# Larger loads, fewer buffers, one output tile: a weighted sum of expert outputs on one core

## The chip, the cores and the metric

The kernel runs on one core of a Trainium2 chip. The metric is the device time of one execution in microseconds (us): the median of three runs of the kernel before is 721.33 us, with runs from 721.21 to 722.09. The profile that is read below is one execution taken by the hardware profiler; its span is 720.4 us. In its lines DVE is VectorE, ACT is ScalarE, POOL is GpSimd and SP is SyncE; a "q" behind an engine's name (SPq) is the part of the engine that issues its transfers, and q1, q10 and q0 are the DMA queues of SyncE, ScalarE and GpSimd.

## The reference

For each of 16 x 1024 = 16384 tokens there are the outputs of 8 experts, each a vector of 512 float32 values, and 8 weights. The result is the weighted sum of the 8 vectors.

```python
batch, seq, n_experts, expert_dim = 16, 1024, 8, 512

def reference(expert_outputs, combine_weights):
    weights = combine_weights[..., np.newaxis]
    return np.sum(expert_outputs * weights, axis=2).astype(np.float32)
```

268.4 MB of expert outputs and 0.5 MB of weights are read and 33.6 MB are written. There is no reuse: every value of the input is multiplied once and added once.

## The kernel before

The tokens are spread over 128 partitions. A step takes 256 tokens, J = 2 neighbouring tokens in each partition, so a load is 4 MiB: one row of 32 KiB (2 tokens x 8 experts x 512 x 4 bytes) for each partition. Loads go alternately to the queues of SyncE and ScalarE, three steps ahead, into four buffers. The 8 KB of weights of a step are loaded by GpSimd, into four small buffers. The output of a step goes to one of four output tiles and is stored on the queue that did not load this step.

```python
in_pool = ctx.enter_context(tc.tile_pool(name="in_pool", bufs=4))
w_pool = ctx.enter_context(tc.tile_pool(name="w_pool", bufs=4))
out_pool = ctx.enter_context(tc.tile_pool(name="out_pool", bufs=4))
prod_pool = ctx.enter_context(tc.tile_pool(name="prod_pool", bufs=2))
...                                        # ES = 4, K_TAIL = 2, LA = 3
load_engines = [nc.sync, nc.scalar]

def issue_load(m):
    in_t = in_pool.tile([P, J, E, D], fp32, name="in_t")
    w_t = w_pool.tile([P, J, E], fp32, name="w_t")
    if m < n_steps - K_TAIL:
        load_engines[m % 2].dma_start(out=in_t, in_=eo_blk[m])
    else:                                  # the last two steps: a transfer for each j
        ...
    nc.gpsimd.dma_start(out=w_t, in_=w_blk[m])
```

The sum of a token is a chain of eight VectorE instructions on 128 x 512 float32 values: a multiply (line 77 in the profile), and then seven times a fused multiply and add (line 83).

```python
for n in range(n_steps):
    if n + LA < n_steps:
        issue_load(n + LA)
    if n >= n_steps - K_TAIL:
        continue
    acc = out_pool.tile([P, J, D], fp32)
    for j in range(J):
        nc.vector.tensor_scalar_mul(out=acc[:, j, :], in0=in_tile[:, j, 0, :],
                                    scalar1=w_tile[:, j, 0:1])
        for e in range(1, E):
            nc.vector.scalar_tensor_tensor(
                out=acc[:, j, :], in0=in_tile[:, j, e, :],
                scalar=w_tile[:, j, e : e + 1], in1=acc[:, j, :],
                op0=mybir.AluOpType.mult, op1=mybir.AluOpType.add)
    load_engines[(n + 1) % 2].dma_start(out=o_blk[n], in_=acc)
```

In the last two steps the work is shared: ScalarE multiplies experts 4 to 7 into bf16 products, VectorE sums experts 0 to 3 and then adds the products, and each j is stored on its own. The buffers synchronise themselves: a tile taken from a pool may be written once all that used its buffer before, a store that reads it among them, has ended.

Of the kernel before, what the change touches and what calls it, by code (L numbers as in the profile page):

```python
# [1 line left out]

# [4 lines left out]


@with_exitstack  # L10
def kernel(
    ctx: ExitStack,
    tc: tile.TileContext,
    expert_outputs: bass.AP,
    combine_weights: bass.AP,
    out: bass.AP,
):
    nc = tc.nc
    fp32 = mybir.dt.float32
    bf16 = mybir.dt.bfloat16  # L20

    B, S, E, D = expert_outputs.shape
    T = B * S
    P = 128
    J = 2
    n_steps = T // (P * J)

    eo_blk = expert_outputs.rearrange("b s e d -> (b s) e d").rearrange(
        "(n p j) e d -> n p j e d", p=P, j=J
    )  # L30
    w_blk = combine_weights.rearrange("b s e -> (b s) e").rearrange(
        "(n p j) e -> n p j e", p=P, j=J
    )
    o_blk = out.rearrange("b s d -> (b s) d").rearrange(
        "(n p j) d -> n p j d", p=P, j=J
    )

    in_pool = ctx.enter_context(tc.tile_pool(name="in_pool", bufs=4))
    w_pool = ctx.enter_context(tc.tile_pool(name="w_pool", bufs=4))
    out_pool = ctx.enter_context(tc.tile_pool(name="out_pool", bufs=4))  # L40
    prod_pool = ctx.enter_context(tc.tile_pool(name="prod_pool", bufs=2))

    ES = E // 2
    K_TAIL = 2

    load_engines = [nc.sync, nc.scalar]

    LA = 3
    in_tiles: list[bass.AP | None] = [None] * n_steps
    w_tiles: list[bass.AP | None] = [None] * n_steps  # L50

    def issue_load(m: int) -> None:
        in_t = in_pool.tile([P, J, E, D], fp32, name="in_t")
        w_t = w_pool.tile([P, J, E], fp32, name="w_t")
        if m < n_steps - K_TAIL:
            load_engines[m % 2].dma_start(out=in_t, in_=eo_blk[m])
        else:
            for j in range(J):
                load_engines[m % 2].dma_start(out=in_t[:, j], in_=eo_blk[m, :, j])
        nc.gpsimd.dma_start(out=w_t, in_=w_blk[m])  # L60
        in_tiles[m] = in_t
        w_tiles[m] = w_t

    for m in range(min(LA, n_steps)):
        issue_load(m)

    for n in range(n_steps):
        if n + LA < n_steps:
            issue_load(n + LA)
        if n >= n_steps - K_TAIL:  # L70
            continue
        in_tile = in_tiles[n]
        w_tile = w_tiles[n]
        acc = out_pool.tile([P, J, D], fp32)

        for j in range(J):
            nc.vector.tensor_scalar_mul(  # L77
                out=acc[:, j, :],
                in0=in_tile[:, j, 0, :],
                scalar1=w_tile[:, j, 0:1],  # L80
            )
            for e in range(1, E):
                nc.vector.scalar_tensor_tensor(  # L83
                    out=acc[:, j, :],
                    in0=in_tile[:, j, e, :],
                    scalar=w_tile[:, j, e : e + 1],
                    in1=acc[:, j, :],
                    op0=mybir.AluOpType.mult,
                    op1=mybir.AluOpType.add,
                )  # L90

        load_engines[(n + 1) % 2].dma_start(out=o_blk[n], in_=acc)  # L92

    tail_steps = list(range(n_steps - K_TAIL, n_steps))
    tail_accs = {}
    tail_prods = {}
    for n in tail_steps:
        acc = out_pool.tile([P, J, D], fp32, name="acc")
        prods = prod_pool.tile([P, J, E - ES, D], bf16, name="prods")
        tail_accs[n] = acc  # L100
        tail_prods[n] = prods

    for j in range(J):
        for n in tail_steps:
            in_tile = in_tiles[n]
            w_tile = w_tiles[n]
            acc = tail_accs[n]
            prods = tail_prods[n]

            for e in range(ES, E):  # L110
                nc.scalar.mul(  # L111
                    out=prods[:, j, e - ES, :],
                    in_=in_tile[:, j, e, :],
                    mul=w_tile[:, j, e : e + 1],
                )
            nc.vector.tensor_scalar_mul(  # L116
                out=acc[:, j, :],
                in0=in_tile[:, j, 0, :],
                scalar1=w_tile[:, j, 0:1],
            )  # L120
            for e in range(1, ES):
                nc.vector.scalar_tensor_tensor(  # L122
                    out=acc[:, j, :],
                    in0=in_tile[:, j, e, :],
                    scalar=w_tile[:, j, e : e + 1],
                    in1=acc[:, j, :],
                    op0=mybir.AluOpType.mult,
                    op1=mybir.AluOpType.add,
                )
            nc.vector.tensor_add(  # L130
                out=prods[:, j, 0:2, :],
                in0=prods[:, j, 0:2, :],
                in1=prods[:, j, 2:4, :],
            )
            nc.vector.tensor_add(  # L135
                out=prods[:, j, 0, :], in0=prods[:, j, 0, :], in1=prods[:, j, 1, :]
            )
            nc.vector.tensor_add(  # L138
                out=acc[:, j, :], in0=acc[:, j, :], in1=prods[:, j, 0, :]
            )  # L140
            nc.sync.dma_start(out=o_blk[n, :, j], in_=acc[:, j, :])


# [1 line left out]
_INS = ['expert_outputs', 'combine_weights']  # L145
_OUTS = [((16, 1024, 512), 'float32')]


# [23 lines left out]
```

## Time and profile before

| what | value |
|---|---|
| time, median of 3 | 721.33 us |
| span of the profiled execution | 720.4 us |
| VectorE busy | 644.4 us, 1020 instructions |
| ScalarE busy | 11.4 us |
| bytes moved | 302.63 MB, mean 420 GB/s |
| load of 4 MiB, issue to landing | 33.3 us (SyncE), 33.5 us (ScalarE) |
| store of 512 KB, issue to landing | 33.4 us (SyncE), 33.5 us (ScalarE) |
| weights of a step, issue to landing | 6.9 us |
| last stores of 256 KB, issue to landing | 3.0 us |

A group of instructions in the page reads: line, engine, operation, what it writes and reads, shape and count, then the busy time in us and the mean duration of one in ns, then the idle time of the engine just before such instructions and what ended most of it. Successive VectorE instructions overlap a little, so that the busy time is less than count times duration. In the table of stretches a row has the stretch and its length, the busy time and count of VectorE, ScalarE and GpSimd, the clock of TensorE (not used here), the share of time in which the 16 DMA engines were busy, and what they moved in GB/s. The "chain of waits" follows the work that ended last back to what released it, step by step.

### The profile page before, as it was taken

What the parts mean: (1) busy time and instruction counts of PE and PEld (TensorE: products, weight loads), DVE (VectorE), ACT (ScalarE), POOL (GpSimd) and SP (SyncE); (2) the same over time, 40 slices, a digit from 0 to 9 for tenths busy, and PEclk for the clock granted to TensorE, in tenths of its full rate; (3) what the DMA queues carried; (4) which work ended last, traced back from release to release, by engine and by line L of the source; (5) the groups of instructions that cost most, each with busy time, mean ns of one, the idle gap of its engine ahead of it and who ended that gap; (6) DMA issues with size and microseconds to landing.
All of it is one profiled execution on the core that took longest, in us unless ns stands there. A gap on an engine that the chain in (4) does not pass through costs nothing.

```text
span 720.4 us, 1532 instructions
## 1 busy us (share of the span) xinstructions
DVE 644.4 (89%) x1020; ACT 11.4 (2%) x17; POOL 35.8 (5%) x68
## 2 busy tenths in 40 slices
DVE  0799999999998999989998999989998999999977
ACT  0000000000000000000000000000000000000023
POOL 1000000000000000000000000000000000000000
DMA  9999999999999999999999999999999999999993
GB/s 380 437 416 451 427 426 430 427 424 439 443 431 426 426 423 431 438 436 434 431 423 426 435 430 442 432 424 427 430 429 432 442 431 428 430 425 428 433 359 120
DMA packets 21068, 302.63 MB, mean 420 GB/s; under 512 B 3136, under 2 KB 4160, under 8 KB 12608
## 3 DMA queue, kind: packets, MB, share of 16 engines
q1 hardware_dynamic: 9792, 151.52, 49.2%
q10 hardware_dynamic: 9216, 150.47, 48.9%
q0 software_dynamic: 2048, 0.53, 0.3%
q14 instruction: 12, 0.10, 0.0%
HBM read 268.96 MB, written 33.55 MB: 420 GB/s over the span
## 4 chain that ended last, share of the span: by engine, by line
DMA 63%; DVE 35%; issue 1%; DVEq 0%; SPq 0%
DMA out_dram<-acc 56%; DVE acc L83 30%; DMA in_t<-in_expert_outputs_dram 8%; DVE acc L77 3%; DVE acc L122 1%; DVE acc L138 0%; DVE prods L130 0%; DVE acc L116 0%; DVE prods L135 0%; DVEq L77 0%; DVEq L116 0%; SPq L92 0%
## 5 line engine op out<-in xcount | busy, mean ns | idle before, releaser
L83 DVE SCALAR_TENSOR_TENSOR acc<-in_t,w_t,acc 128x512 f32<-128x512 f32 x868 | 580.1, 743 | 0.0
L77 DVE TENSOR_SCALAR acc<-in_t,w_t 128x512 f32<-128x512 f32 x124 | 54.6, 482 | 66.3 <-DMA in_t<-in_expert_outputs_dram 43.4
L60 POOL DMA_DIRECT2D w_t<-in_combine_weights_dram x64 | 35.6, 556 | 637.7 <-DVE acc L83 636.9
L111 ACT ACT_TABLE_LOAD x1 | 1.3, 1283 | 690.6 <-DMA in_t<-in_expert_outputs_dram 690.6
L111 ACT ACTIVATE prods<-in_t,w_t 128x512 bf16<-128x512 f32 x16 | 10.1, 709 | 9.0 <-DMA in_t<-in_expert_outputs_dram 9.0
L122 DVE SCALAR_TENSOR_TENSOR acc<-in_t,w_t,acc 128x512 f32<-128x512 f32 x12 | 8.9, 745 | 0.0
L116 DVE TENSOR_SCALAR acc<-in_t,w_t 128x512 f32<-128x512 f32 x4 | 1.9, 481 | 5.3 <-DMA out_dram<-acc 5.3
L138 DVE TENSOR_TENSOR acc<-acc,prods 128x512 f32<-128x512 f32 x4 | 2.8, 688 | 0.0
L130 DVE TENSOR_TENSOR prods<-prods 128x1024 bf16<-128x1024 bf16 x4 | 2.7, 683 | 0.0
L135 DVE TENSOR_TENSOR prods<-prods 128x512 bf16<-128x512 bf16 x4 | 1.7, 417 | 0.0
L156 POOL MEMSET const-float32-0.0<- 128x1 f32 x1 | 0.1, 99 | 0.2 <-issue 0.2
L156 POOL MEMSET const-bfloat16-1.0<- 128x1 bf16 x1 | 0.1, 102 | 0.0
L156 POOL MEMSET const-float32-1.0<- 128x1 f32 x1 | 0.1, 99 | 0.0
L156 POOL MEMSET const-uint8-127<- 128x1 uint8 x1 | 0.1, 99 | 0.0
## 6 DMA issues: line engine op xcount, KB each, us to landing
in_t<-in_expert_outputs_dram ACTq DMA_DIRECT2D x31, 4096.0 KB, 33.5
in_t<-in_expert_outputs_dram SPq DMA_DIRECT2D x31, 4096.0 KB, 33.3
out_dram<-acc ACTq DMA_DIRECT2D x31, 512.0 KB, 33.5
out_dram<-acc SPq DMA_DIRECT2D x31, 512.0 KB, 33.4
in_t<-in_expert_outputs_dram SPq DMA_DIRECT2D x2, 2048.0 KB, 31.2
in_t<-in_expert_outputs_dram ACTq DMA_DIRECT2D x2, 2048.0 KB, 13.9
w_t<-in_combine_weights_dram POOLq DMA_DIRECT2D x64, 8.0 KB, 6.9
out_dram<-acc SPq DMA_DIRECT2D x4, 256.0 KB, 3.0
```

Source lines behind the costliest of these rows:

```text
L60: nc.gpsimd.dma_start(out=w_t, in_=w_blk[m])
L77: nc.vector.tensor_scalar_mul(out=acc[:, j, :], in0=in_tile[:, j, 0, :], scalar1=w_tile[:, j, 0:1],)
L83: nc.vector.scalar_tensor_tensor(out=acc[:, j, :], in0=in_tile[:, j, e, :], scalar=w_tile[:, j, e : e + 1], in1=acc[:, j, :], op0=mybir.Al ...
L111: nc.scalar.mul(out=prods[:, j, e - ES, :], in_=in_tile[:, j, e, :], mul=w_tile[:, j, e : e + 1],)
L116: nc.vector.tensor_scalar_mul(out=acc[:, j, :], in0=in_tile[:, j, 0, :], scalar1=w_tile[:, j, 0:1],)
L122: nc.vector.scalar_tensor_tensor(out=acc[:, j, :], in0=in_tile[:, j, e, :], scalar=w_tile[:, j, e : e + 1], in1=acc[:, j, :], op0=mybir.Al ...
L130: nc.vector.tensor_add(out=prods[:, j, 0:2, :], in0=prods[:, j, 0:2, :], in1=prods[:, j, 2:4, :],)
L135: nc.vector.tensor_add(out=prods[:, j, 0, :], in0=prods[:, j, 0, :], in1=prods[:, j, 1, :])
L138: nc.vector.tensor_add(out=acc[:, j, :], in0=acc[:, j, :], in1=prods[:, j, 0, :])
L156: nc = _bacc.Bacc("TRN2", target_bir_lowering=False, num_devices=1)
```

## The change

- A chunk is now 512 tokens, J = 4 in each partition, and a load is 8 MiB, one row of 64 KiB for each partition. All loads go to SyncE's queue. There are three input buffers, and two chunks are loaded ahead.
- All weights are loaded once, at the start, by ScalarE's queue, into one tile: 8 rows of 512 bytes for each partition.
- The first multiply of each token moves from VectorE to ScalarE. VectorE does seven fused operations for each token.
- There is one output tile instead of four. To give VectorE something to do while the store of the chunk before still reads that tile, the first token of a chunk is summed in place, in its input buffer; only its last operation writes to the output tile. ScalarE does the first multiply of the next chunk (`first`) ahead of issuing the store.
- The last seven loads are cut into pieces that become smaller, down to one expert of one token for each partition in the very last, so that the sum can follow the data closely. The bf16 products of the last steps go.

The three input buffers (64 KiB for each partition), the output tile (8 KiB) and the weights (4 KiB) take 204 KiB for each partition.

```diff
-    J = 2
-    n_steps = T // (P * J)
+    K = 16
+    J = 4
+    N = T // (P * K)
...
+    x = expert_outputs.rearrange("b s e d -> (b s) e d").rearrange(
+        "(n p k) e d -> n p (k e) d", p=P, k=K
+    )
+    w = combine_weights.rearrange("b s e -> (b s) e").rearrange(
+        "(n p k) e -> p n (k e)", p=P, k=K
+    )
...
-    in_pool = ctx.enter_context(tc.tile_pool(name="in_pool", bufs=4))
-    w_pool = ctx.enter_context(tc.tile_pool(name="w_pool", bufs=4))
-    out_pool = ctx.enter_context(tc.tile_pool(name="out_pool", bufs=4))
-    prod_pool = ctx.enter_context(tc.tile_pool(name="prod_pool", bufs=2))
+    in_pool = ctx.enter_context(tc.tile_pool(name="in_pool", bufs=3))
+    w_pool = ctx.enter_context(tc.tile_pool(name="w_pool", bufs=1))
+    out_pool = ctx.enter_context(tc.tile_pool(name="out_pool", bufs=1))
...
+    chunks = [(n, k) for n in range(N) for k in range(0, K, J)]
+    last = len(chunks) - 1
...
+    def cuts(i):
+        if i == last:
+            return (0, 4, 8, 12, 16, 20, 24, 26, 28, 29, 30, 31, 32)
+        if i == last - 1:
+            return tuple(range(0, J * E + 1, 4))
+        if i >= last - 3:
+            return tuple(range(0, J * E + 1, 8))
+        if i >= last - 6:
+            return (0, 16, 32)
+        return (0, J * E)
...
+    def load(i):
+        n, k = chunks[i]
+        t = in_pool.tile([P, J * E, D], fp32, name="in_t")
+        in_tiles[i] = t
+        at = cuts(i)
+        for a, b in zip(at, at[1:]):
+            nc.sync.dma_start(out=t[:, a:b], in_=x[n, :, k * E + a : k * E + b])
...
+    def first(i):
+        n, k = chunks[i]
+        t = in_tiles[i]
+        pin(nc.scalar.mul(out=t[:, 0], in_=t[:, 0], mul=w_t[:, n, k, 0:1]))
...
+    def rest(i):
+        n, k = chunks[i]
+        t = in_tiles[i]
+        acc = out_pool.tile([P, J, D], fp32, name="acc")
+        for j in range(1, J):
+            pin(
+                nc.scalar.mul(out=acc[:, j], in_=t[:, j * E], mul=w_t[:, n, k + j, 0:1])
+            )
+        if i < last:
+            first(i + 1)
         for j in range(J):
...
+            part = t[:, 0] if j == 0 else acc[:, j]
             for e in range(1, E):
                 nc.vector.scalar_tensor_tensor(
...
+                    out=acc[:, j] if e == E - 1 else part,
+                    in0=t[:, j * E + e],
+                    scalar=w_t[:, n, k + j, e : e + 1],
+                    in1=part,
+                    op0=mult,
+                    op1=add,
                 )
+        if i < last:
+            pin(nc.scalar.dma_start(out=o[n, :, k : k + J], in_=acc))
+        else:
+            for a, b in ((0, 2), (2, 3), (3, 4)):
+                nc.sync.dma_start(out=o[n, :, k + a : k + b], in_=acc[:, a:b])
...
+    AHEAD = 2
+    load(0)
+    nc.scalar.dma_start(out=w_t.rearrange("p n k e -> p n (k e)"), in_=w)
+    for i in range(1, AHEAD):
+        load(i)
+    first(0)
+    for i in range(len(chunks)):
+        if i + AHEAD <= last:
+            load(i + AHEAD)
+        rest(i)
```

`pin` keeps ScalarE's instructions in the order in which the program has them.

More of the change, by code (lines that the diff above doesn't have):

```diff
@@ L19 @@
     fp32 = mybir.dt.float32
-    bf16 = mybir.dt.bfloat16
+    mult, add = mybir.AluOpType.mult, mybir.AluOpType.add
     B, S, E, D = expert_outputs.shape
@@ L24 @@
     P = 128
-    J = 2
-    n_steps = T // (P * J)
-    eo_blk = expert_outputs.rearrange("b s e d -> (b s) e d").rearrange(
-        "(n p j) e d -> n p j e d", p=P, j=J
-    )
-    w_blk = combine_weights.rearrange("b s e -> (b s) e").rearrange(
-        "(n p j) e -> n p j e", p=P, j=J
-    )
-    o_blk = out.rearrange("b s d -> (b s) d").rearrange(
-        "(n p j) d -> n p j d", p=P, j=J
-    )
-    in_pool = ctx.enter_context(tc.tile_pool(name="in_pool", bufs=4))
-    w_pool = ctx.enter_context(tc.tile_pool(name="w_pool", bufs=4))
@@ L40 @@
-    out_pool = ctx.enter_context(tc.tile_pool(name="out_pool", bufs=4))
-    prod_pool = ctx.enter_context(tc.tile_pool(name="prod_pool", bufs=2))
[L43 to L74, printed above, removed]
-        for j in range(J):
[L77 to L81, printed above, removed]
+    K = 16
@@ new lines @@
+    J = 4
+    N = T // (P * K)
+    x = expert_outputs.rearrange("b s e d -> (b s) e d").rearrange(
+        "(n p k) e d -> n p (k e) d", p=P, k=K
+    )
+    w = combine_weights.rearrange("b s e -> (b s) e").rearrange(
+        "(n p k) e -> p n (k e)", p=P, k=K
+    )
+    o = out.rearrange("b s d -> (b s) d").rearrange("(n p k) d -> n p k d", p=P, k=K)
+    in_pool = ctx.enter_context(tc.tile_pool(name="in_pool", bufs=3))
+    w_pool = ctx.enter_context(tc.tile_pool(name="w_pool", bufs=1))
@@ new lines @@
+    out_pool = ctx.enter_context(tc.tile_pool(name="out_pool", bufs=1))
+    w_t = w_pool.tile([P, N, K, E], fp32, name="w_t")
+    chunks = [(n, k) for n in range(N) for k in range(0, K, J)]
+    last = len(chunks) - 1
+    in_tiles = {}
+    pin = tc.keep_in_program_order
+    def cuts(i):
[8 more added lines that the diff above has]
+        return (0, J * E)
@@ L82 @@
             for e in range(1, E):
                 nc.vector.scalar_tensor_tensor(
[L84 to L89, printed above, removed]
-                )
-        load_engines[(n + 1) % 2].dma_start(out=o_blk[n], in_=acc)
-    tail_steps = list(range(n_steps - K_TAIL, n_steps))
-    tail_accs = {}
@@ L96 @@
[L96 to L141, printed above, removed]
```

## The prediction

> **What bounds the kernel now.** I read the page's busy shares first, then the table of stretches, then the chain of waits, and last the DMA queues of three short stretches, because the question of this change turned out to be how queues share the DMA engines.
>
> ```profile
> span 720.4 us, 1532 instructions
> DVE 644.4 (89%) x1020; ACT 11.4 (2%) x17; POOL 35.8 (5%) x68
> ...
> HBM read 268.96 MB, written 33.55 MB: 420 GB/s over the span
> ...
> DMA out_dram<-acc 56%; DVE acc L83 30%; DMA in_t<-in_expert_outputs_dram 8%; DVE acc L77 3%; DVE acc L122 1%; DVE acc L138 0%; DVE prods L130 0%; DVE acc L116 0%; DVE prods L135 0%; DVEq L77 0%; DVEq L116 0%; SPq L92 0%
> ...
> L83 DVE SCALAR_TENSOR_TENSOR acc<-in_t,w_t,acc 128x512 f32<-128x512 f32 x868 | 580.1, 743 | 0.0
> L77 DVE TENSOR_SCALAR acc<-in_t,w_t 128x512 f32<-128x512 f32 x124 | 54.6, 482 | 66.3 <-DMA in_t<-in_expert_outputs_dram 43.4
> ```
>
> VectorE is 89% busy, but it is not the bound. Its idle time stands in front of the multiply that opens a token, and it waits there for loads and for stores. The stretches say the same:
>
> ```profile
> 150.00:640.00 490.00, 450.66 (x710) 0.00 (x0) 24.10 (x45) 1.00 1.01 431
> ...
> 680.00:720.40 40.40, 29.94 (x50) 11.41 (x17) 0.00 (x0) 1.00 0.66 260
> ```
>
> From 150 to 640 us the DMA engines are full (share 1.01) at 431 GB/s. All bytes at that rate take 302.5 MB / 431 GB/s = 702 us; the other 18 us of the span are a slow start and a tail. So the store waits in the chain are only the saturated DMA seen through a buffer. With four output tiles and four input tiles nobody needs a store soon.
>
> Now the queues. The first block is 156 to 159 us, when one hardware queue holds a load and the other a store; the second is 10 to 16 us, when both hold loads and GpSimd's queue holds the weights (columns: packets, MB, share of the 16 engines).
>
> ```profile
> q1 hardware_dynamic: 32, 1.05, 80.9%
> q10 hardware_dynamic: 32, 0.13, 10.6%
> ```
>
> ```profile
> q10 hardware_dynamic: 42, 1.38, 53.1%
> q1 hardware_dynamic: 35, 1.15, 44.2%
> q0 software_dynamic: 34, 0.01, 0.6%
> ```
>
> 32 packets against 32, although the bytes stand 8 to 1: a packet is one row (32 KiB per partition of a load, 4 KiB of a store), and the queues take turns by packet, not by byte. The start shows it again. The first three weight loads land at 10.4, 15.4 and 20.3 us (issue plus time to landing), 5.0 us apart. Each has a data packet and a completion packet on every engine. Each packet waits for a 32 KiB packet of both other queues: 2 x 2 x 32 KiB / (431/16 GB/s) = 4.9 us.
>
> **What the skill says.** The Trainium skill, "DMA: Bandwidth & Descriptors", section "Queues, rings and completion order", says each DMA engine goes round the queues that have work and switches only between packets. The trace agrees: 32 to 32, and 5.0 us measured against 4.9. The same page, "Measured (HBM→SBUF, 128 partitions, SWDGE, issued from GpSimd)", has 425 GB/s for 16 MB against 341 for 1 MB. That speaks for large loads, but the 4 MiB loads here already reach 431, so 8 MiB have little left to win. "ScalarE: Activation LUTs", section "What ACT_TABLE_LOAD costs", gives about 1283 ns; the trace has 1283.
>
> **The change part by part.**
>
> Bytes: unchanged, so 702 us remains the floor of a full DMA.
>
> Instructions: the 124 + 4 multiplies leave VectorE for ScalarE (128 x 0.71 us = 91 us, by the 706 ns of its multiplies in the tail), and the bf16 tail goes. VectorE keeps 128 tokens x 7 = 896 fused operations. Fourteen of them take 9.28 us in the chain, 0.663 each, so 594 us in all, or 28 x 0.663 = 18.6 us per chunk of four tokens. There are 32 chunks. A chunk's DMA work is 8 MiB + 1 MiB = 9.44 MB, 21.9 us. With nothing else in the way the DMA would still be the bound.
>
> Output tile: this is the step that decides. There is one, and all of it must be stored before ScalarE or VectorE may write the next chunk's. Summing the first token in place lets VectorE do only six operations (4.0 us) before it needs the tile. So the store must land within 4 us of its issue. Its issue comes at the end of chunk i, on ScalarE's queue, and at that moment the input buffer of chunk i comes free and the load of chunk i+3 is issued on SyncE's queue. The two go packet by packet. Per engine the store has 8 packets of 8 KiB (0.30 us each at 26.9 GB/s), the load 8 packets of 64 KiB (2.43 us each). Every store packet follows one load packet: 8 x (2.43 + 0.30) = 21.9 us, and about 2.0 us from issue to landing (a tail store of 256 KB took 2.0 alone) makes 23.9. So store and load end together.
>
> Period of a chunk: 23.9 from the end of one chunk to its store's landing, 0.15 for the wake-up, then the remaining 22 operations, 14.6 us: 38.7 us, of which VectorE idles 20. The DMA is then not full: 9.44 MB in 38.7 us are 244 GB/s.
>
> Start: the weights are now one transfer of 128 x 8 rows of 512 B on ScalarE's queue, 64 packets per engine if each row is one. Three loads, 24 packets per engine, stand on the other queue at once. Turn about, only 24 weight packets get through while the loads take 24 x 2.43 = 58 us; the rest follow quickly. Weights at about 63 us; then a multiply and 18.6 us: chunk 0 ends at 82.5, where before the first sum began at 22.9.
>
> Middle: chunks 1 to 22 stand against whole 64 KiB rows: 22 x 38.7 = 851 us. End: the last loads are cut, their packets are shorter and the store gets more turns. Three chunks against 32 KiB rows: store 8 x (1.22 + 0.30) + 2 = 14.2 (say 14.5), period 29.3, 88 us. Two against 16 KiB: 9.3, period 24.1, 48 us. Two against about 8 KiB: 7.0, period 21.7, 43 us. Two with no load left: 2.4 + 2, period 19.2, 38 us. The last store and the end of the program: 4 us.
>
> Sum: 82.5 + 851 + 88 + 48 + 43 + 38 + 4 = 1155 us.
>
> The shrinking last loads save what they are made for: the tail of before, at 260 GB/s over 40.4 us, lost (1 - 260/431) x 40.4 = 16 us. That doesn't weigh against 20 us of idling in each of 22 chunks.
>
> **The rivals.**
>
> (a) The queues share by bytes after all. Then a store needs 2 x 2.44 + 2 = 6.9 us, the period is 21.7, just under the 21.9 of the full DMA, and the change does what it is for: 702 + some 8 = about 710 us. This is what the cover of six operations looks made for. Against it stand the 32-to-32 stretch and the weights 5.0 us apart.
>
> (b) A 64 KiB row goes as two packets of 32 KiB. Nothing in the trace has such a row, 32 KiB is the longest it shows. The store then takes 14.5 us as in the chunks of 32 KiB rows, 25 periods are 29.3 us: 732 + 48 + 43 + 38 + 82.5 + 4 = 948 us.
>
> (c) The weights' 512 B rows are bundled, say eight to a packet. GpSimd's queue does that with its 64 B rows (34 packets for 0.01 MB), the hardware queues give each row of 2 KiB or more its own. Then they land with the first load at about 24 us, and 40 us come off: 1115.
>
> (d) VectorE becomes the bound: no, 594 us are less than 702.
>
> **Range and chances.** The mechanism (turns by packet, one output tile, 4 us of cover) rests on measured stretches; I give it about nine in ten. Within it (b) has perhaps one in eight and (c) one in four. The completion packet may cost one turn more or less, 2.4 us x 22 = 54 us. I predict 1145 us, between the sum and (c), and 1020 to 1220 as the range that should hold it 8 times in 10. Faster by over 2% needs (a) with every bit of the tail's gain: 0.06. Within 2%: 0.04. Slower by over 2%: 0.90.
>
> **What would show it.** In the profile of the changed kernel: VectorE busy near 600 us but only about 52% of the span, with six operations, a gap near 20 us that ends on a store, then 22 operations; stores landing about 24 us after issue in the middle, and shorter ones at the end; packets of the two queues equal in number, with a load packet of 64 KiB; mean DMA rate near 260 GB/s; the first sum at about 63 us, released by the weights. I am wrong if stores land in under 8 us beside a load (then a), if loads have twice the packets (then b), or if the first sum starts near 24 us (then c). If the DMA share stays at 1.0 in the middle, the whole argument has failed.

## The result, and the profile after

| | before | after |
|---|---|---|
| time, median of four | 721.68 us | 1226.37 us |
| span of the profiled execution | 720.4 us | 1225.9 us |
| VectorE busy | 644.4 us, 89% | 621.7 us, 51% |
| mean DMA rate | 420 GB/s | 247 GB/s |
| store, issue to landing | 33.4 us (512 KB) | 24.8 us (1 MiB) |

The ratio of the times is 1.70, with a 95% interval of 1.698 to 1.702: the change makes the kernel 70% slower. The prediction was 1145 us, range 1020 to 1220, so the direction and the mechanism are as predicted, and the time lies 6 us above the range. The sum of its steps, 1155 us, is 71 us short. The rest of this document is about whether the mechanism is the one that was named, and about those 71 us.

First the page of the changed kernel: the busy shares, the DMA in 40 slices, the chain of waits, and two groups of VectorE's operations.

```profile
span 1225.9 us, 1324 instructions
DVE 621.7 (51%) x896; ACT 83.2 (7%) x129; POOL 0.2 (0%) x4
...
DMA  9934764377346744674367445753575476688671
...
HBM read 268.96 MB, written 33.55 MB: 247 GB/s over the span
...
DMA out_dram<-acc 52%; DVE acc L91 38%; DMA in_t<-in_expert_outputs_dram 2%; DVE in_t L91 2%; ACT acc L84 0%; ACT L76 0%; SPq L71 0%; ACT in_t L76 0%; DVEq L91 0%; ACTq L84 0%; ACTq L76 0%
...
L91 DVE SCALAR_TENSOR_TENSOR acc<-in_t,w_t 128x512 f32<-128x512 f32 x32 | 24.0, 751 | 527.7 <-DMA out_dram<-acc 527.7
L91 DVE SCALAR_TENSOR_TENSOR in_t<-in_t,w_t 128x512 f32<-128x512 f32 x192 | 143.9, 750 | 68.2 <-ACT in_t L76 63.9
```

Before, the DMA row was nines from end to end; now it goes up and down. The same row before:

```profile
DMA  9999999999999999999999999999999999999993
```

All but some 13 us of VectorE's idle time stands in two places. 527.7 us stand in front of the 32 operations with which the first token of a chunk enters the output tile, ended by a store each time. The other 63.9 us are the start, until ScalarE's first multiply. That a store stands at 56% in the chain before and at 52% now means two things: before, it was a full DMA seen through buffers; now the engines move nothing for much of the time.

The chain over one chunk, in order of time (start, length, what):

```profile
82.59 24.97 DMA out_dram<-acc
107.56 0.03 issue
107.61 0.04 issue
107.65 10.72 DVE acc L91 x16
118.38 0.02 issue
118.40 0.76 DVE acc L91
...
122.33 0.76 DVE acc L91
123.12 24.80 DMA out_dram<-acc
```

Store, then VectorE, then the next store, nothing beside it on the chain: one chunk takes 123.12 - 82.59 = 40.5 us. The same time from the side of the engines (stretch, length, busy time and count of VectorE, ScalarE and GpSimd, clock, DMA share, GB/s):

```profile
84.00:106.00 22.00, 3.01 (x5) 0.00 (x0) 0.00 (x0) 1.00 0.91 391
108.00:122.00 14.00, 13.82 (x21) 2.14 (x4) 0.00 (x0) 1.00 0.00 0
```

While the store is under way VectorE stands, and while VectorE works the DMA moves nothing at all. The two take turns where they should overlap.

The DMA queues from 90 to 100 us, and then from 20 to 30 us (q1 holds the loads; q10 holds a store in the first stretch and the weights in the second):

```profile
q1 hardware_dynamic: 53, 3.47, 80.1%
q10 hardware_dynamic: 52, 0.43, 10.0%
```

```profile
q1 hardware_dynamic: 82, 4.33, 101.0%
q10 hardware_dynamic: 82, 0.04, 1.6%
```

53 packets against 52 and 82 against 82: turns by packet. A packet of a load is 3.47 MB / 53 = 65.5 KB, a whole row of 64 KiB; a packet of the weights is 0.04 MB / 82, one row of 512 bytes. (In the second stretch 16 of q1's 82 packets are the completion packets of a load, 4 bytes each.)

A stretch counts a packet where it starts. The 391 GB/s above leave out most of the load's first rows, which start at 83.5 to 84 us, and 10 us are not a whole number of turns. From 86.5 to 105.5 us there are seven whole turns:

```profile
q1 hardware_dynamic: 112, 7.34, 89.2%
q10 hardware_dynamic: 112, 0.92, 11.4%
```

That is 435 GB/s: the engines are full while the two queues take turns.

### The profile page after: what moved, and what is told of

It is laid out like the page before. It is cut to its first block, busy times and chain, and to the rows that moved or that the text cites. A ratio compares the mean times of both kernels' runs of the same rounds, so it can differ in the third digit from the quotient of the medians.

```text
span 1225.9 us, 1324 instructions
## 1 busy us (share of the span) xinstructions
DVE 621.7 (51%) x896; ACT 83.2 (7%) x129; POOL 0.2 (0%) x4
## 4 chain that ended last, share of the span: by engine, by line
DMA 55%; DVE 40%; another core or an unknown queue 3%; issue 2%; ACT 0%; SPq 0%; DVEq 0%; ACTq 0%
DMA out_dram<-acc 52%; DVE acc L91 38%; DMA in_t<-in_expert_outputs_dram 2%; DVE in_t L91 2%; ACT acc L84 0%; ACT L76 0%; SPq L71 0%; ACT in_t L76 0%; DVEq L91 0%; ACTq L84 0%; ACTq L76 0%
## 5 line engine op out<-in xcount | busy, mean ns | idle before, releaser
L91 DVE SCALAR_TENSOR_TENSOR acc<-in_t,w_t,acc 128x512 f32<-128x512 f32 x672 | 464.9, 746 | 5.3
L91 DVE SCALAR_TENSOR_TENSOR acc<-in_t,w_t 128x512 f32<-128x512 f32 x32 | 24.0, 751 | 527.7 <-DMA out_dram<-acc 527.7
L91 DVE SCALAR_TENSOR_TENSOR in_t<-in_t,w_t 128x512 f32<-128x512 f32 x192 | 143.9, 750 | 68.2 <-ACT in_t L76 63.9
L84 ACT ACTIVATE acc<-in_t,w_t 128x512 f32<-128x512 f32 x96 | 62.3, 711 | 1064.4 <-DMA out_dram<-acc 1064.4
L76 ACT ACTIVATE in_t<-in_t,w_t 128x512 f32<-128x512 f32 x32 | 22.6, 707 | 38.8 <-DMA w_t<-in_combine_weights_dram 38.8
L76 ACT ACT_TABLE_LOAD x1 | 1.3, 1283 | 23.1 <-DMA in_t<-in_expert_outputs_dram 23.1
## 6 DMA issues: line engine op xcount, KB each, us to landing
out_dram<-acc ACTq DMA_DIRECT2D x31, 1024.0 KB, 24.8
in_t<-in_expert_outputs_dram SPq DMA_DIRECT2D x4, 256.0 KB, 13.7
w_t<-in_combine_weights_dram ACTq DMA_DIRECT2D x1, 512.0 KB, 62.4
```

The lines of the kernel that those rows point to most:

```text
L76: pin(nc.scalar.mul(out=t[:, 0], in_=t[:, 0], mul=w_t[:, n, k, 0:1]))
L84: nc.scalar.mul(out=acc[:, j], in_=t[:, j * E], mul=w_t[:, n, k + j, 0:1])
L91: nc.vector.scalar_tensor_tensor(out=acc[:, j] if e == E - 1 else part, in0=t[:, j * E + e], scalar=w_t[:, n, k + j, e : e + 1], in1=part, ...
```

## The experiments

The theory: a store and a load on different queues go packet by packet, so a store with short rows lasts as long as the load beside it, and the single output tile makes VectorE wait for that. The rivals: the loads as such (64 KiB rows, 256 KiB apart) are slow; the single tile is the loss whatever its store does; turn-taking is the loss whatever waits for it.

### The store's queue

```diff
-            pin(nc.scalar.dma_start(out=o[n, :, k : k + J], in_=acc))
+            nc.sync.dma_start(out=o[n, :, k : k + J], in_=acc)
```

> The stores go out on SyncE's queue, behind the load that was issued before and ahead of the load that the freed buffer allows; nothing else in the program's text changes (the order in which VectorE works off two tokens shifts with it). If the loss comes from stores taking turns packet by packet with 64 KiB rows of another queue, a store now waits for whole loads ahead of it only and needs about 4.5 us once it is at the head; the period of a chunk falls from 40.4 to between 21.9 (full DMA) and 23.1 us (4.5 us of store plus 28 operations of VectorE), and the time to 760 to 820 us. If the loss is the single output tile whatever queue its store takes, or the loads themselves (64 KiB rows, 256 KiB apart), the time stays above 1100 us.

Measured: 816.36 us, ratio to before 1.131 (1.129 to 1.134). One word in the program takes away 410 of the 505 us lost. The DMA issues of this run (queue, count, KB each, us to landing):

```profile
out_dram<-acc SPq DMA_DIRECT2D x31, 1024.0 KB, 4.8
```

4.8 us in place of 24.8, with the same tile, the same rows and the same loads: neither the tile by itself nor the loads are the cause. VectorE's order shifts, too: all 28 operations of a period now stand ahead of the store, so that nothing covers it and VectorE waits 4.9 us for each. The period is 23.7 us (successive wake-ups of VectorE at 300.68 and 324.34), near the 23.1 of the expectation. Of the 95 us that remain against the kernel before, 41 are the late start (first sum at 64 us, not 22.9).

### The weights' place

```diff
-    load(0)
-    nc.scalar.dma_start(out=w_t.rearrange("p n k e -> p n (k e)"), in_=w)
+    nc.sync.dma_start(out=w_t.rearrange("p n k e -> p n (k e)"), in_=w)
+    load(0)
```

> The weights are loaded ahead of everything on SyncE's queue. If their 512-byte rows wait one turn each for a row of a load, they land within about 4 us now, the first sum starts at about 26 us in place of 64 us, and the whole kernel is 36 to 40 us faster: about 1188 us. If the 62.4 us of the weights' transfer are its own (1024 short rows), it delays the first load by as much and the time doesn't fall, or rises to 1240 us and more.

Measured: 1190.63 us, 36 us less than the change; the theory said 36 to 40. A later run with the same edit shows the transfer itself at 4.4 us from issue to landing, against 62.4 us behind the loads' rows. The start is as predicted.

### The length of the loads' rows

Every load is cut into eight pieces of 8 KiB per partition; only the last chunk keeps its own cut.

```diff
-        if i == last - 1:
-            return tuple(range(0, J * E + 1, 4))
         ...
-        return (0, J * E)
+        return tuple(range(0, J * E + 1, 4))
```

> Every load is cut into eight of 8 KiB per partition; bytes, tiles and queues stay. If the turns go by packet, a store's 8 packets now wait for 8 packets of 8 KiB, not 64 KiB: it lands in 7 to 8 us (the last chunks of the changed kernel show 7.7), the period falls to about 24 us, the weights land at about 22 us, and the time is 770 to 830 us. If the size of the rows plays no part, stores keep some 25 us and the time stays near 1226 us; more transfers could only make it longer.

Measured: 839.97 us, ratio 1.164.

```profile
out_dram<-acc ACTq DMA_DIRECT2D x31, 1024.0 KB, 8.5
```

Stores land in 8.5 us, not 24.8, with the same bytes on the same two queues. The time is 10 us above the expected span. The store is half a microsecond longer than I put it, and nearly all of VectorE's 22 operations run at the slower spacing of the next section: successive stores are issued at 299.80 and 325.34, a period of 25.5 us in place of 24. (The next load is issued at 308.29 here, when the store has landed; the pieces that the store meets are those of the load before.) That eight times as many, smaller transfers make this kernel 386 us faster is the plainest sign of what a long row does to its neighbour.

### VectorE's order

In the chain above, 16 operations take 10.72 us, 0.67 each, and the six behind them 0.79 each. The order of VectorE's instructions is not the one of the program text: the framework interleaves two tokens where it can, and these six belong to one token, each adding to the result of the one before. In the last chunks it does something else as well (start, length, engine, line, operation):

```profile
1029.27 0.74 DVE L91 SCALAR_TENSOR_TENSOR in_t<-in_t,w_t 128x512 f32<-128x512 f32 x1
1029.94 0.74 DVE L91 SCALAR_TENSOR_TENSOR acc<-in_t,w_t,acc 128x512 f32<-128x512 f32 x1
...
1035.90 0.74 DVE L91 SCALAR_TENSOR_TENSOR in_t<-in_t,w_t 128x512 f32<-128x512 f32 x1
1036.56 0.74 DVE L91 SCALAR_TENSOR_TENSOR acc<-in_t,w_t,acc 128x512 f32<-128x512 f32 x1
1037.34 0.37 ACTq L100 DMA_DIRECT2D out_dram<-acc  x1
```

The in-place operations of the next chunk (`in_t`) run in front of the store, between the last operations of this one. They no longer cover the store: they delay it. Two runs fix the order, with the first token's seven operations ahead in both.

```diff
-        for j in range(J):
-            part = t[:, 0] if j == 0 else acc[:, j]
-            for e in range(1, E):
-                nc.vector.scalar_tensor_tensor(...)
+        for j, e in [(0, e) for e in range(1, E)] + [
+            (j, e) for e in range(1, E) for j in range(1, J)
+        ]:
+                part = t[:, 0] if j == 0 else acc[:, j]
+                pin(nc.vector.scalar_tensor_tensor(...))
```

> VectorE's order is fixed: the six in-place operations of the first token, its last, then the other three tokens in turn (expert 1 of each, expert 2 of each, and so on), in every chunk. If an operation that needs the result of the one just before it starts 0.787 us after it, and one that doesn't 0.663, the 22 operations behind the store take 14.6 us in place of 15.5, and in the last chunks the six operations are again hidden behind the store: period 39.6 us in the middle and about 1180 us in all. If the slower spacing has another cause (the DMA, ScalarE at the same time), the middle stays at 40.4 us and only the last chunks get shorter: about 1200 us.

The other pins the loop as it stands (token by token):

> VectorE's order is fixed too, but as the program has it: every operation needs the result of the one before. If that is what the spacing of 0.787 us comes from, the 22 operations behind the store take 17.3 us and the period in the middle is 42.3 us; in the last chunks the six in-place operations are hidden behind the store. In all about 1262 us, 75 us above the interleaved order, from the same operations. If the spacing has another cause, the time equals that of the interleaved order within 1%, 1185 us.

Measured: 1185.36 us interleaved, 1257.25 us token by token: 72 us apart, 75 expected, by order alone. Interleaved, VectorE wakes at 504.01 and again at 543.54, a period of 39.5 us. The same group of operations in the two runs, interleaved first:

```profile
L92 DVE SCALAR_TENSOR_TENSOR acc<-in_t,w_t,acc 128x512 f32<-128x512 f32 x672 | 448.0, 746 | 0.0
```

```profile
L91 DVE SCALAR_TENSOR_TENSOR acc<-in_t,w_t,acc 128x512 f32<-128x512 f32 x672 | 499.6, 751 | 20.4
```

The mean of one hardly differs (746 and 751 ns), but 672 of them cover 448.0 us in one order and 499.6 in the other, with 20.4 us of small gaps: neighbours that don't depend on each other overlap more. A mean duration times a count can't show that.

### One tile or two

So that two output tiles take the space of the change's one, these runs halve everything: two tokens in each partition, six input buffers of 32 KiB, tiles of 4 KiB, VectorE token by token. They differ in one digit.

```diff
-    out_pool = ctx.enter_context(tc.tile_pool(name="out_pool", bufs=1))
+    out_pool = ctx.enter_context(tc.tile_pool(name="out_pool", bufs=2))
```

One tile:

> Half the size of everything: two tokens in each partition, loads of 4 MiB with 32 KiB rows into six buffers (the same 192 KiB), one output tile of 4 KiB, VectorE in the order of the program; loads and stores on two queues as in the change. A store's 8 packets of 4 KiB take turns with 32 KiB rows and land in about 13.8 us (as in the run with two queues), then come 8 operations of VectorE, 6.2 us: a period of 20 us, 64 times, with the weights at 63 us: about 1310 us. If a store wait of this kind grows with the size of the chunk only, it is about half as long for half the size and the time stays below 1000 us.

Two tiles:

> The same with two output tiles of 4 KiB (together what the change has in one), and no other difference. A store must then land before the second chunk after it writes, 2 x 12 us later, and does: the loads fill the DMA at about 400 GB/s (what the engines move while one queue has loads and the other stores), so 75 us of start and 277 MB, about 770 us. If it is the turn-taking itself that costs, and not the single tile that waits for it, the time stays above 1100 us.

Measured: 1241.25 us with one tile, 771.49 us with two. Stores in the second land no sooner:

```profile
out_dram<-acc ACTq DMA_DIRECT2D x63, 512.0 KB, 13.7
```

```profile
out_dram<-acc ACTq DMA_DIRECT2D x63, 512.0 KB, 15.6
```

13.7 us with one tile and 15.6 with two. So turn-taking alone costs little; it costs when something waits for the slow transfer. With one tile the period is 20.1 us (wake-ups at 408.37 and 428.44), as expected; the sum of 1310 us was too high, because I counted every chunk at that, and nine of the 63 stores, all of them against the short last rows, cost no wait. With two tiles the number came out by luck. I had counted on 400 GB/s; the engines were full from 100 to 600 us, at 428:

```profile
100.00:600.00 500.00, 469.90 (x636) 60.04 (x90) 0.00 (x0) 1.00 1.00 428
```

What set the time was nearly as much VectorE: it started at 64 us, waited for stores for 11.5 us in all, and otherwise worked token by token to the end of the span, 769.5 us.

### Repairing the change

This run has stores on SyncE's queue, weights first, and VectorE interleaved (token by token in the last chunk). The last three stores stay on ScalarE's queue.

```diff
-            pin(nc.scalar.dma_start(out=o[n, :, k : k + J], in_=acc))
+            eng = nc.sync if i < last - 3 else nc.scalar
+            pin(eng.dma_start(out=o[n, :, k : k + J], in_=acc))
```

> Stores on SyncE's queue (on ScalarE's in the last chunks, where rows are short), weights first, VectorE interleaved. The store (4.8 us) is then hidden behind the six operations (4.7 us), VectorE needs 19.4 us for a chunk, and the DMA is the bound. If one queue can fill the engines as the two of the kernel before do (431 GB/s), the time is 702 + 10 = 712 us. If one queue holds only the 415 GB/s that the first slices of the changed kernel show, it is 729 + 10 = 739 us. If something else holds the stores, over 790 us.

Measured: 752.8 us, ratio 1.043 (1.042 to 1.045); neither 712 nor 739. The stretches say where the difference is:

```profile
100.00:600.00 500.00, 429.11 (x628) 56.46 (x89) 0.00 (x0) 1.00 1.00 425
600.00:700.00 100.00, 85.27 (x126) 12.63 (x20) 0.00 (x0) 1.00 1.00 420
700.00:751.00 51.00, 45.80 (x66) 4.51 (x7) 0.00 (x0) 1.00 0.29 115
```

The DMA is full to 700 us, as it should be, and then VectorE works for another 45.8 us. A store on this queue lies behind a load that was issued earlier, VectorE needs the tile and waits for it, and so it runs about two chunks behind the loads. While the DMA is the bound that costs nothing; at the end the two chunks, twice 19 us, remain. I had put down 10 us of tail.

The next run splits each load and each store into halves on two queues:

```diff
+            for eng, a, b in ((nc.sync, 0, 16), (nc.scalar, 16, 32)):
+                pin(eng.dma_start(out=t[:, a:b], in_=x[n, :, k * E + a : k * E + b]))
...
+                pin(nc.sync.dma_start(out=o[n, :, k : k + 2], in_=acc[:, 0:2]))
+                pin(nc.scalar.dma_start(out=o[n, :, k + 2 : k + 4], in_=acc[:, 2:4]))
```

> As the kernel with one queue, but the two halves of a load (32 KiB rows) go to SyncE's and ScalarE's queues, and so do the two halves of a store, each ahead of the next load on its queue. If two queues are what brings 431 GB/s, the time is about 712 us, a little under the kernel before; if the rate hangs on the layout (rows 256 KiB apart), it stays at 735 to 740 us.

Measured: 903.3 us, a miss: I had brought back the fault that I was studying.

```profile
out_dram<-acc SPq DMA_DIRECT2D x29, 512.0 KB, 2.7
out_dram<-acc ACTq DMA_DIRECT2D x28, 512.0 KB, 13.8
```

SyncE's half is issued 1.3 us sooner (316.01 against 317.34) and lands in 2.7 us. SyncE's queue then goes on to its half of the next load, and ScalarE's half of the store takes turns with that load's 32 KiB rows: 13.8 us.

Last in this line, the parts of the change without the single tile and with one queue: two tokens in each partition, five input buffers, four output tiles, weights first, shrinking last loads, VectorE interleaved.

> The change's parts without the single tile and without a second queue for the stores: two tokens in each partition, five input buffers, four output tiles, weights first, loads and stores on SyncE's queue, shrinking last loads. Nothing waits for a store but the DMA itself; at the 425 GB/s that one queue showed, 712 us and 4 us of weights and 6 us of tail: about 722 us, equal to the kernel before. If VectorE still runs chunks behind the loads at the end, 740 us or more.

Measured: 727.73 us, ratio 1.008 (1.007 to 1.010).

```profile
100.00:600.00 500.00, 427.71 (x634) 65.02 (x91) 0.00 (x0) 1.00 1.01 431
```

From 100 to 600 us one queue fills the DMA at 431 GB/s with rows of 32 KiB, just as the two queues before. The last 36 us run at 181 GB/s: the tail was not shortened, and the change's parts bring nothing over the kernel before.

### The tail of the kernel before

Since the floor of a full DMA is 702 us, the kernel before can only gain in its tail. One edit takes the last step's loads off ScalarE's queue:

```diff
-                load_engines[m % 2].dma_start(out=in_t[:, j], in_=eo_blk[m, :, j])
+                nc.sync.dma_start(out=in_t[:, j], in_=eo_blk[m, :, j])
```

> The kernel before with one edit: the loads of the last step go out on SyncE's queue, and so not behind a multiply of ScalarE that waits for the step before (in the profile before they are issued at 690.7 us, though their buffer was free at 673.5). If that wait is what leaves the DMA at 260 GB/s in the last 40 us, some 10 us come off: 708 to 713 us. If the tail is long for its arithmetic and stores, it stays at 721 us.

Measured: 720.87 us, ratio 0.9991 (0.9983 to 0.9999): a miss. The DMA filled up as intended, 431 GB/s from 690 to 696 us where it had 276, but the last piece is seen by ScalarE at 707.6 us, where it was 708.4. Between 702 and 708 us the engines move only 68 GB/s. This is one engine that is still at work. The rate from 703 to 708 us, in slices of 0.125 us (the burst in the middle is a store):

```profile
GB/s 0 33 131 0 0 0 0 33 131 0 0 0 0 131 0 0 0 0 131 0 344 328 377 475 393 181 0 0 131 0 0 0 0 33 33 33 33 0 33 33
```

131 GB/s in one slice are 16.4 KB, one row of the last pieces, and such a row comes every 0.6 to 0.8 us; the trace has 0.61 us for one. From 700.1 to 707.2 us ten such rows follow one another, never two at a time. So the bytes were not all in at 702 us, as my next expectation still says: a mean over 16 engines hides one that is late. With that edit kept, the two loops of the tail are exchanged, so that VectorE takes the pieces in the order of landing:

```diff
-    for j in range(J):
-        for n in tail_steps:
+    for n in tail_steps:
+        for j in range(J):
```

> As the run with the tail loads on SyncE's queue, and in the last two steps the loop runs over steps first and tokens second, so that VectorE takes the pieces in the order in which they land (62 first, 62 second, 63 first, 63 second). In the run before this one all bytes of the loads were in at about 702 us and VectorE then had 13 us of work left, after waiting 4.8 us for the first piece of step 63 while the second of step 62 already lay there. If that order is what the tail is long for, only the last piece (about 4 us of VectorE, 3 us of store) is left at 702: 709 to 713 us. If the tail is VectorE's arithmetic whatever its order, it stays at 720 us.

Measured: 718.65 us, ratio 0.9961 (0.9947 to 0.9974). This is the fastest version of the study, 0.4% under the kernel before. Only the last piece is now left at the end, but it is there at 707.5 us, not at 702; from there on work and store take 10 us, where I had put 7.

The late engine falls behind over the whole run. Each transfer ends with 16 completion packets, as many as there are engines. On SyncE's queue in the kernel before, the last of the 16 comes 0.8 us after the eighth at 63 us and 6.6 us after it at 666 us. It gets there in eight steps of 0.7 to 0.9 us, with nothing in between. The page of that kernel has one more queue:

```profile
q14 instruction: 12, 0.10, 0.0%
```

Eleven of its packets (8 KiB, 0.31 us each) fall into the run ahead of the tail. The steps follow those at 56.8, 137.1, 213.4, 301.9, 379.3, 467.9, 545.5 and 633.9 us, each in the first transfer that is completed after the packet; the other three, at 323.8, 345.8 and 433.3 us, bring no step. So the lag goes with the fetching of the program's own instructions. That is a coincidence in time, eight times over; no run changed these fetches.

## Why the prediction was right, and where it was wrong

**Turns by packet, and the single tile: right, and shown.** The packets in the stretches are equal in number. Stores fall from 24.8 to 4.8 us with another queue and to 8.5 us with shorter rows. One tile or two makes 1241 or 771 us. Neither half is enough alone: with two tiles, slow stores did no harm; with quick stores, one tile left 95 us, 41 of them the late start.

**The start: right.** The weights arrive at 63 us and chunk 0 ends at 82.59 us, 82.5 predicted. Rival (c), bundled rows, is out (82 packets against 82), and moving the weights took away 36 us. Rival (b) is out too: a row of 64 KiB is one packet. Rival (a), turns by bytes, is out with 24.8 us for a store in place of 6.9.

**The step that failed is the period of a chunk, 23.9 + 0.15 + 14.6 = 38.7 us.** The mechanism in it is right, and its size is not. The period is 40.5 us (972.9 - 82.6 over 22 chunks), and 22 x 1.8 = 39 us of the missing 71 are in it. Two terms were too small.

- The store's landing, 24.8 us in place of 23.9. The eight turns are as predicted: in every chunk of the middle one takes 2.72 to 2.74 us, against 2.73. What is too small is the fixed part, 2.0 us, which I took from a store that had the engines to itself; here it is 3.0. In the store issued at 82.59 us the load's first row starts 1.1 us after the issue and takes 3.2 us, not 2.4; the last engine is done 0.8 us after the middle one; and 0.5 us later the store counts as landed. These are 3.2 us on top of eight turns.
- VectorE's 22 operations, 15.5 us in place of 14.6. The spacing of 0.663 us was measured where two tokens alternate. Six of the 22 wait for each other, at 0.787. The interleaved run shows this term by itself: its period is 39.5 us. What is left of the difference to 38.7 is the store's.

**The second step that failed is "End", 221 us, which is 253 us (from 972.9 to the end).** I assumed that the six in-place operations always follow the store's issue, as the program reads. In the last chunks they precede it. With the order fixed, the span falls by 42 us: 20 in the middle, where 22 x 0.95 = 21 are expected, and 24 at the end, which then takes 229 us (from 954.2 to 1183.5), with 1 us lost at the start. The 8 us that are left between 229 and 221 were not taken apart.

**The range.** The rivals that I weighed all lay below the sum, so I put the point 10 us under it, and gave the sum room for one turn more or less only. Every term that I then got wrong was too short. Both durations came from easier conditions than those of the new loop: VectorE's spacing from two tokens that alternate, the store's fixed part from engines with nothing else to do. The range should have reached further up than down.

## What to carry to other kernels

When two transfers share the DMA engines on different queues, compare their rows, not their bytes: the one with short rows gets one of them through for each row of the other, so a small store or a table of weights lasts as long as the big load beside it. If anything waits for such a transfer, put it on the load's queue ahead of the load, shorten the load's rows, or give it another buffer so that nothing waits. And when a buffer is given up for larger transfers, count what the one that remains now has to wait for. To read a rate, take a stretch of whole turns, and where a transfer ends late, look whether one engine is behind the rest.

## What the hardware did that I had not expected

- An operation on VectorE that adds to the result of the one just before it starts 0.787 us after it, one that doesn't 0.663 (128x512 float32). Over 672 operations the order alone made 448.0 or 499.6 us.
- One queue holds the full rate: 431 GB/s with 32 KiB rows and stores in line with loads, as much as two queues.
- Turns between two queues cost the engines nothing: 435 GB/s over seven turns of a 64 KiB row and an 8 KiB row, 2.72 us each.
- One of the 16 DMA engines fell 6.6 us behind the others in the course of the kernel before, in eight steps of 0.7 to 0.9 us, each after an instruction fetch of 8 KiB; the last piece of the loads waited for it.
